# Sixteen blocks of a late modulation, issued from other places of an encoder kernel's first stage

## The chip, the cores and the metric

The kernel runs on one core of a Trainium2 chip. What counts is the device time of one execution in microseconds, the median of several runs. The core has five engines that matter here, each with its own in-order instruction stream: TensorE (PE, with its weight loads as PEld), VectorE (DVE), ScalarE (ACT), GpSimd (POOL) and SyncE (SP), whose queue issues every DMA of this kernel.

## The reference, cut to what matters

An encoder of two layers over 1024 rows of width 1024, in float32. Each layer's input is a normalised x, scaled and shifted by a modulation that comes from one vector c; a gate of the same origin weighs the layer's output:

```
c_act = silu(c)
mod = c_act @ ada_w[i] + ada_b[i]              # one row of 3072 for each layer i
shift, scale, gate = split(mod, 3)
h = rms_norm(x, norm_g[i]) * (1 + scale) + shift
out = layer_ab(h, ...) if i == 0 else layer_diff(h, ...)
x = x + gate * out
```

layer_ab projects h: to a query latent (384 columns) and a key/value latent (256), each of which is normalised later by a row's own root mean square, to a rotary key (32), to queries, keys and values of a stick-breaking attention (512 each) and to gates z (1024). Two attentions follow, then the output projection. Only layer 0's shift and scale are needed at once. Layer 1's shift and scale and both layers' gates are needed much later: they are the late modulation, 4 x 1024 dot products of length 1024, 16 MB of weights.

## The kernel before, in words

Activations lie transposed in SBUF, features on the 128 partitions and 512 rows to a half. Every float32 matrix is split into a high and a low part, and a product is three matmuls (lines 172 to 174): high by high, low by high, high by low. A weight block of 128 output columns is loaded to w_st, cast to w_hi on ACT and its rest taken to w_lo on POOL (wprep, line 153 for the subtraction); dense_fm then runs two halves of 8 x 3 matmuls into a PSUM bank and calls an evacuation. Three score banks (sc) and two dense banks (psd) go round.

The stage around the change, in the order of the code: the first half of the rows is normalised, modulated and multiplied by the five latent blocks (to line 592); then the second half (latent_evac writes both parts of a latent to memory, lat_h and lat_l); the rotary table cs is made on DVE (lines 629 to 636); the rotary key's block (krt, line 698) is projected; the two norms of the latents follow (latent_norm: sums on POOL and PE, an inverse root by Newton steps on DVE, rl in the names, and row_out, which turns the result to a row and writes it: rq_d for the queries, rkv_d for keys and values). The query row is read back to all partitions (rqb), and DVE makes two scaled tables te and to from it and cs, which are written to tq_d. The rotated key is written to krot_d; the code calls this DMA `turned`. Then four gate blocks zb are projected through the score banks, with ACT's sigmoid and a product on DVE (line 250); zb and te share buffers. After that begins the stick-breaking attention: the first query/key block goes to the two dense banks, is split by ACT (qk_a) and DVE (qk_k, line 153), and three DMAs rearrange its halves (qk_b, qk_k, qk_a); meanwhile the values (wv) are projected.

The late modulation is the generator ada_rest: sixteen steps, each of which loads a block of 1 MB (ada_st, two times 1024 columns) into one of six buffers of the tag ld, takes two dots on DVE (line 522, one ISA instruction and the reading of its accumulator) and adds the bias (line 677, into gt for the gates, n = 0, or modc for layer 1's shift and scale, n = 1). `more(n)` advances it by n steps. A scheduler then orders each engine's instructions by its own estimates and the data they depend on. `with tc.issue_after(x):` adds that what the block traces on x's engine stands behind x on that engine; where x is a DMA, it binds DMAs of SP alone, and dots on DVE are not held by it. Before, steps are advanced by four behind `turned` and by four behind each of the first three gate blocks.

Of the kernel before, what the change touches and what calls it, by code (L numbers as in the profile page):

```python
# [21 lines left out]
P = 128  # L22
# [3 lines left out]
NT = S // P  # L26
# [45 lines left out]
def kernel(ctx, tc, a, out):  # L72
    nc = tc.nc
    mm = nc.tensor.matmul

    def dma(dst, src):
        dst = dst.bitcast(F32) if dst.dtype == F32R else dst
        src = src.bitcast(F32) if src.dtype == F32R else src
        return nc.sync.dma_start(dst, src)
# [34 lines left out]
    tq_d = dram.tile([2, P, S], F32, name="tq_d")  # L114
    rq_d = dram.tile([NT, P], F32, name="rq_d")
    rkv_d = dram.tile([NT, P], F32, name="rkv_d")
    krot_d = dram.tile([P, S], F32, name="krot_d")
# [58 lines left out]
    def dense_fm(w, rhs, evac, bank=None):  # L176

        wh, wl = (t.rearrange("p (k c) -> p k c", c=P) for t in w)
        nk = len(rhs)
        for half in range(2):  # L180
            ps = (bank or d_bank)()
            sl = slice(half * 512, half * 512 + 512)
            for k in range(nk):
                mm3(ps, wh[:, k, :], wl[:, k, :], rhs[k][0][:, sl], rhs[k][1][:, sl], k == 0, k == nk - 1)
            evac(ps, half, sl)

    def rstd_cols(pool, ss, n, scale, eps, name, extra=None, bufs=2):

        h, r, t = (pool.tile([P, n], F32, name=name + x, tag=name + x, bufs=bufs) for x in "hrt")
        if extra is None:  # L190
            nc.vector.tensor_scalar(h, ss, scale, eps, op0=ALU.mult, op1=ALU.add)
        else:
            nc.vector.scalar_tensor_tensor(t, extra, eps, extra, op0=ALU.mult, op1=ALU.mult)
            nc.vector.scalar_tensor_tensor(h, ss, scale, t, op0=ALU.mult, op1=ALU.add)
        ri = r.bitcast(I32)
        nc.vector.tensor_scalar(ri, h.bitcast(I32), 1, None, op0=ALU.logical_shift_right)
        nc.vector.tensor_scalar(ri, ri, -1, 0x5F3759DF, op0=ALU.mult, op1=ALU.add)
        nc.vector.tensor_scalar(h, h, -0.5, None, op0=ALU.mult)
        for _ in range(3):
            nc.vector.tensor_mul(t, r, r)  # L200
            nc.vector.tensor_mul(t, t, h)
            nc.vector.scalar_tensor_tensor(r, t, 1.5, r, op0=ALU.add, op1=ALU.mult)
        return r

    def row_out(pool, cols, n, dst, bank):

        tr = bank()
        nc.tensor.transpose(tr[0:n, 0:P], cols, identf)
        row = pool.tile([16, P], F32, name="row", tag="row", bufs=2)
        nc.vector.tensor_copy(row[0:n], tr[0:n, 0:P])  # L210
        dma(dst, row[0:n])

    def row_bc(src, n):

# [14 lines left out]
    def row_sums(tile_of, nt, bank):  # L229

        ps = bank()
        for t in range(nt):
            mm(ps[:, t:t + 1], tile_of(t), ones, start=True, stop=True)  # L233
        return ps[:, 0:nt]
# [242 lines left out]
    with tc.tile_pool(name="a0", bufs=1, reuse_waits="tile") as a0:  # L477
# [10 lines left out]
        def ada_load(k):  # L488
            ada_st[k] = a0.tile([P, 2, D], F32, name="ada_st", tag="ld", bufs=NLD)
            return dma(ada_st[k].rearrange("p i d -> p (i d)"), a["ada_t"][k - 1] if k else a["ada_0"])  # L490

        def wide(name, tag):
            return a0.tile([P, S], F32, name=name, tag=tag, bufs=4)
# [23 lines left out]
        def dots(st):  # L517

            m = a0.tile([P, 2], F32, name="adm", tag="adm", bufs=4)
            for n in range(2):  # L520
                junk = a0.tile([P, D], F32, name="junkd", tag="junkd")
                nc.vector.tensor_tensor_reduce(junk, st[:, n, :], cb, op0=ALU.mult, op1=ALU.add, scale=1.0, scalar=0.0,
                                               accum_out=m[:, n:n + 1])
            return m
# [8 lines left out]
        def x_mod(g, k, xts, lo):  # L533

            tr = t_bank()
            for j in range(4):
                nc.tensor.transpose(tr[:, j * P:(j + 1) * P], xts[j][:, k * P:(k + 1) * P], identf)
            hf = a0.tile([P, 512], F32, name="hf", tag="hf", bufs=3)
            sl = slice(g * 512, g * 512 + 512)
            nc.scalar.activation(hf, tr, AF.Identity, scale=gsc[0][:, k:k + 1], bias=modc[0][:, k:k + 1])  # L540
            hi = nc.scalar.copy(hT[k][0][:, sl], hf)
            return sub(lo, hT[k][1][:, sl], hf, hT[k][0][:, sl].bitcast(F32)), hi
# [38 lines left out]
        for k in range(KC):  # L581
            if k + 1 < KC:
                known = ada_block(k + 1)
                _, done = x_mod(0, k + 1, x0, "vec")
                if k + 4 < KC:
                    held = ada_load(k + 4)
# [22 lines left out]
        for k in range(KC):  # L609
            ready, _ = x_mod(1, k, x1, "vec")  # L610
# [56 lines left out]
        def ada_rest():  # L667
            bias = adab.rearrange("p (i n) -> p i n", n=8)
            for n in range(2):
                dst, b_ = ((gt, bias[:, 2::3, :]), (modc[1], bias[:, 3:5, :]))[n]  # L670
                dst = dst.rearrange("p (i n) -> p i n", n=8)
                for k in range(KC):
                    st = a0.tile([P, 2, D], F32, name="ada_st", tag="ld", bufs=NLD)
                    with tc.issue_after((turned if n or k > 1 else held).ins):
                        dma(st.rearrange("p i d -> p (i d)"), a["ada_r"][n, k])
                    with tc.issue_after(turned.ins):
                        nc.vector.tensor_tensor(dst[:, :, k], dots(st), b_[:, :, k], op=ALU.add)
                    yield k
        rest = ada_rest()

        def more(n):
            for _ in range(n):
                next(rest, None)

        def latent_norm(b0, n, row_d):
            part = lambda half, b: sqt[half, b // 2][:, b % 2 * 512:b % 2 * 512 + 512]
            for half in range(2):
                for b in range(b0 + 1, b0 + n):
                    nc.gpsimd.tensor_tensor(part(half, b0), part(half, b0), part(half, b), op=ALU.add)
            ss = row_sums(lambda t: part(t // 4, b0)[:, t % 4 * P:t % 4 * P + P], NT, v_bank)  # L690
            r = rstd_cols(a0, ss, NT, 1.0 / (n * P), 1e-6, "rl")
            row_out(a0, r, NT, row_d, v_bank)


        krt = wide("krt", "a")
# [3 lines left out]
        with tc.issue_after(held.ins):  # L699
            wkr = wprep(a["w0"][21])  # L700
        dense_fm(wkr, hT, kr_evac, s_bank)
        latent_norm(0, 3, rq_d)
        latent_norm(3, 2, rkv_d)
        rqb = wide("rqb", "b")
        dma(rqb, row_bc(rq_d, P))
# [4 lines left out]
        to = wide("to", "a")  # L710
        nc.vector.tensor_mul(to[0:64], rqb[0:64], cs[0:64])
        nc.vector.tensor_copy(to[64:128], rqb[64:128])
        dma(tq_d[1], to)
        krc = wide("krc", "b")
        for qd in range(4):
            o = qd ^ 1
            nc.scalar.copy(krc[32 * qd:32 * qd + 32], krt[32 * o:32 * o + 32])
        nc.gpsimd.tensor_tensor(krt, krt, krc, op=ALU.add)
        turned = dma(krot_d, krt)
        more(4)  # L720

        for h in range(8):
# [1 line left out]
        for b in range(NZB):  # L724
# [5 lines left out]
            more(4)  # L730
        more(16)
        row_out(a0, gt, 16, gate_d.rearrange("i (n p) -> (i n) p", p=P), t_bank)
        mod_finish(1)

# [141 lines left out]
    for h in range(8):  # L876
# [29 lines left out]
        def mla_mid(par):  # L906
            c1 = slice(4 * par, 4 * par + 4)
            rl = mp.tile([P, 4], F32, name="rl", tag="rl", bufs=2)
            if not seq:
                nc.vector.tensor_tensor(lst[:, 4 * par + 2:4 * par + 4], lst[:, 4 * par + 2:4 * par + 4],  # L910
                                        lst2[:, 2 * par:2 * par + 2], op=ALU.add)
            elif par == 1:
                nc.vector.tensor_tensor(lst[:, 4:8], lst[:, 4:8], lst2, op=ALU.add)
            nc.vector.reciprocal(rl, lst[:, c1])
            row_out(mp, rl, 4, rin_d[h, c1], t_bank)
            rb = mp.tile([P, 512], F32, name="rb", tag="rb", bufs=1)
            dma(halves(rb)[nr[e]], row_bc(rin_d[h, c1], 64))
            z_ = par_view(zt, par, seq)
            nc.gpsimd.tensor_tensor(z_[nr[e]], halves(rb)[nr[e]], z_[nr[e]], op=ALU.mult)
# [206 lines left out]
    with tc.tile_pool(name="e0", bufs=1, reuse_waits="tile") as e0:  # L1126
        fg = e0.tile([P, D], F32, name="fg")
        dma(fg, a["final_g"].to_broadcast([P, D]))
        for t in range(NT):
# [17 lines left out]
            r = rstd_cols(e0, s1, 1, 1.0 / D, 1e-6, "rg")  # L1147
# [93 lines left out]
```

## Time and profile before

| | us |
|---|---|
| median of 3 runs | 1492.08 (1490.76 to 1494.83) |
| the profiled execution | 1493.56 |
| its span | 1491.8 |
| PE busy | 1386.7 (93%) |
| DVE busy | 950.9 (64%) |
| ACT busy | 679.3 (46%) |
| POOL busy | 428.3 (29%) |

The span runs from the first to the last instruction. Busy times are sums over the whole program; what a stage waits for is read from its own stretch. The late modulation lies in the first 190 us: the trace has its dots between 94 and 184 us. "PEclk" is the granted share of TensorE's full clock of 2.4 GHz; 0.5 is its lower level, 1.2 GHz.

### The profile page before, as it was taken

How to read it: one execution, taken by the hardware profiler on the slowest of the kernel's cores; microseconds unless marked ns; L12 is line 12 of the kernel's file. 1: busy time of each engine (PE TensorE's matmuls, PEld its weight loads, DVE VectorE, ACT ScalarE, POOL GpSimd, SP SyncE). 2: the span in 40 equal slices, each digit the busy share in tenths (PEclk: the TensorE clock that was granted, in tenths of full speed). 3: DMA queues.
4: the chain of work that ended last, by engine and by line, in shares of the span. 5: the costliest groups of instructions: out<-in, count | busy, mean ns of one | idle time of the engine just before them, and what ended most of it. 6: DMA issues, size and time to landing. Idle time of an engine off the chain costs nothing.

```text
span 1491.8 us, 20861 instructions
## 1 busy us (share of the span) xinstructions
PE 1386.7 (93%) x7264; PEld 1155.6 (77%) x7264; DVE 950.9 (64%) x2137; ACT 679.3 (46%) x1380; POOL 428.3 (29%) x498
## 2 busy tenths in 40 slices
PE   5999599999998799998879899999999999997797
PEld 4778488888886688887767688888888888886686
DVE  5677947777678865576557426655575656567674
ACT  5742145555555653555345325444444534344321
POOL 2132311322236454635132311132121312134100
PEclk9999899999999999999989999999999999998899
DMA  9536921222243156433746231333232333335262
GB/s 371 225 116 254 365 74 49 67 73 63 62 139 116 58 173 212 145 110 104 238 127 246 57 93 41 78 105 108 64 93 64 101 80 97 85 105 172 81 202 91
DMA packets 110072, 190.38 MB, mean 128 GB/s; under 512 B 8784, under 2 KB 70088, under 8 KB 106896
## 3 DMA queue, kind: packets, MB, share of 16 engines
q1 hardware_dynamic: 109968, 189.05, 40.1%
q8 instruction: 58, 0.95, 0.3%
q14 instruction: 46, 0.38, 0.1%
HBM read 131.75 MB, written 39.27 MB: 115 GB/s over the span
## 4 chain that ended last, share of the span: by engine, by line
PE 39%; DMA 6%; DVE 4%; issue 2%; POOL 2%; ACT 1%; SPq 0%; DVEq 0%; POOLq 0%; ACTq 0%
PE psd L172 7%; PE psd L173 7%; PE psd L174 7%; PE sc L293 4%; PE pv L327 4%; PE sc L172 2%; PE sc L173 2%; PE sc L174 2%; DMA rb<-rst_d 1%; DMA qk_k<-qk_a 1%; DMA w_st<-in_wo_dram 1%; PE pv L233 1%; DMA y_hi<-yh_d 1%; PE tr L307 1%; PE tr L309 1%
## 5 line engine op out<-in xcount | busy, mean ns | idle before, releaser
L153 POOL TENSOR_TENSOR w_lo<-w_st,w_hi 128x1024 fp32r<-128x1024 f32 (+2 forms) x61 | 149.5, 2453 | 369.4 <-ACT w_hi L158 365.5
L153 DVE TENSOR_TENSOR pt_l<-tr,pt_h 128x512 fp32r<-128x512 f32 (+1 forms) x240 | 148.7, 631 | 103.1 <-ACT pt_h L158 90.0
L158 ACT CAST pt_h<-tr 128x512 fp32r<-128x512 f32 (+1 forms) x240 | 125.9, 545 | 131.8 <-PE tr L309 121.4
L174 PE MATMUL psd<-h1h,w_lo 128*128 128x512 f32 x448 | 177.0, 395 | 0.0
L173 PE MATMUL psd<-h1l,w_hi 128*128 128x512 f32 x448 | 176.2, 393 | 0.0
L172 PE MATMUL psd<-h1h,w_hi 128*128 128x512 f32 x448 | 176.0, 393 | 0.0
L172 PE MATMUL psd<-h0h,w_hi 128*128 128x512 f32 x264 | 106.6, 404 | 15.6 <-DVE qk_k L153 15.6
L293 PE MATMUL sc<-qk_k,qk_a 128*128 128x512 f32 (+2 forms) x288 | 104.4, 367 | 2.0 <-DVE st L1056 1.0
L173 PE MATMUL psd<-h0l,w_hi 128*128 128x512 f32 x264 | 106.0, 401 | 0.0
L174 PE MATMUL psd<-h0h,w_lo 128*128 128x512 f32 x264 | 105.1, 399 | 0.0
L158 ACT CAST w_hi<-w_st 128x1024 fp32r<-128x1024 f32 x55 | 57.7, 1050 | 94.3 <-PE psd L173 34.2
L293 PE MATMUL sc<-qk_k,qk_b 128*128 128x512 f32 (+2 forms) x288 | 98.2, 348 | 0.0
L1056 DVE CUSTOM_DVE_ANT_0 g<-sc,tz 128x512 f32<-128x512 f32 (+3 forms) x128 | 72.2, 586 | 40.0 <-PE sc L293 33.9
L173 PEld LDWEIGHTS psd<-h1l,w_hi 128*128 128x128 f32 x448 | 84.2, 188 | 16.9
L174 PEld LDWEIGHTS psd<-h1h,w_lo 128*128 128x128 f32 x448 | 84.2, 188 | 16.2
L172 PEld LDWEIGHTS psd<-h1h,w_hi 128*128 128x128 f32 x448 | 84.2, 188 | 16.1
L1062 ACT ACTIVATE g<-g,st 128x640 f32<-128x640 f32 (+3 forms) x64 | 63.4, 990 | 67.2 <-DVE st L1061 62.4
L327 PE MATMUL pv<-pt_l,vt 128*128 128x256 f32 x320 | 88.7, 303 | 5.1 <-DVE pt_l L153 4.7
L327 PE MATMUL pv<-pt_h,vt 128*128 128x256 f32 x320 | 89.4, 296 | 2.7 <-DVE ot L417 2.7
L776 DVE TENSOR_TENSOR_SCAN g<-g 128x640 f32<-128x640 f32 (+3 forms) x32 | 65.8, 2056 | 20.4 <-ACT g L773 20.4
L172 PEld LDWEIGHTS psd<-h0h,w_hi 128*128 128x128 f32 x264 | 50.5, 191 | 25.6 <-DVE qk_k L153 16.1
L327 PEld LDWEIGHTS pv<-pt_l,vt 128*128 128x128 f32 x320 | 62.6, 196 | 9.1 <-DVE pt_l L153 4.8
(458 smaller groups left out, 3736.5 us busy)
## 6 DMA issues: line engine op xcount, KB each, us to landing
w_st<-in_w_dram SPq DMA_DIRECT2D x43, 512.0 KB
ada_st<-in_ada_r_dram SPq DMA_DIRECT2D x16, 1024.0 KB
w_st<-in_wo_dram SPq DMA_DIRECT2D x16, 512.0 KB
ada_st<-in_ada_t_dram SPq DMA_DIRECT2D x7, 1024.0 KB
yh_d<-yh SPq DMA_DIRECT2D x28, 256.0 KB
yl_d<-yl SPq DMA_DIRECT2D x28, 256.0 KB
w_st<-in_wv_dram SPq DMA_DIRECT2D x12, 512.0 KB
qk_b<-qk_k SPq DMA_DIRECT2D x24, 256.0 KB
```

Of the source, the lines that this page charges most:

```text
L153: return (nc.vector if eng == "vec" else nc.gpsimd).tensor_tensor(out_, x_, y_, op=ALU.subtract)
L158: nc.scalar.copy(hi, src)
L172: mm(ps, sh, mh, start=start, stop=False)
L173: mm(ps, sh, ml, start=False, stop=False)
L174: mm(ps, sl, mh, start=False, stop=stop)
L233: mm(ps[:, t:t + 1], tile_of(t), ones, start=True, stop=True)
L293: mm(ps[:, :nn], st[:, q], mv[:, lo_:lo_ + nn], start=m == 0, stop=not diag and m == len(pairs) - 1)
L307: nc.tensor.transpose(tr[:, P:256], pb[:, (2 * j + 1) * P:(2 * j + 2) * P], identf)
L327: mm(dst, st, tt[w][:, m * 256:m * 256 + 256], start=j == 0 and m == 0 and x == 0, stop=j == n - 1 and m == 1 and x == len(ps_) - 1)
L776: nc.vector.tensor_tensor_scan(ur, ur, ur, 1.0, op0=ALU.mult, op1=ALU.bypass)
L1056: nc.vector.tensor_tensor_reduce(e_[:, sl], ps, tz[:, S - L + sl.start:S - L + sl.stop], op0=ALU.add, op1=ALU.max, scale=1.0, scalar=-3e38 ...
L1062: nc.scalar.activation(e_[:, :L], e_[:, :L], AF.Exp, scale=0.125, bias=st[:, 2 + c:3 + c], accum_out=lst[:, c1:c1 + 1] if c == 0 else st[: ...
```

## The change

Four of the sixteen steps are advanced ahead of the norms, where before none was. Their loads stand behind `held` (the last load of layer 0's modulation) and their adds behind `ready` (the last product of the second half's modulated input, on DVE). The other four of n = 0 have their loads behind the write of the query norm's row (`row_st`), and the eight of n = 1 behind the second table's write (`scaled`); the adds of all twelve stand behind the copy of the query norm's row (`row_cp`), which is on DVE. row_out returns these two instructions.

```diff
--- before.py
+++ after.py
@@ -207,8 +207,7 @@
         tr = bank()
         nc.tensor.transpose(tr[0:n, 0:P], cols, identf)
         row = pool.tile([16, P], F32, name="row", tag="row", bufs=2)
-        nc.vector.tensor_copy(row[0:n], tr[0:n, 0:P])
-        dma(dst, row[0:n])
+        return nc.vector.tensor_copy(row[0:n], tr[0:n, 0:P]), dma(dst, row[0:n])
 
     def row_bc(src, n):
 
@@ -671,9 +670,9 @@
                 dst = dst.rearrange("p (i n) -> p i n", n=8)
                 for k in range(KC):
                     st = a0.tile([P, 2, D], F32, name="ada_st", tag="ld", bufs=NLD)
-                    with tc.issue_after((turned if n or k > 1 else held).ins):
+                    with tc.issue_after((held if n == 0 and k < 4 else row_st if n == 0 else scaled).ins):
                         dma(st.rearrange("p i d -> p (i d)"), a["ada_r"][n, k])
-                    with tc.issue_after(turned.ins):
+                    with tc.issue_after((ready if n == 0 and k < 4 else row_cp).ins):
                         nc.vector.tensor_tensor(dst[:, :, k], dots(st), b_[:, :, k], op=ALU.add)
                     yield k
         rest = ada_rest()
@@ -681,6 +680,8 @@
         def more(n):
             for _ in range(n):
                 next(rest, None)
+
+        more(4)
 
         def latent_norm(b0, n, row_d):
             part = lambda half, b: sqt[half, b // 2][:, b % 2 * 512:b % 2 * 512 + 512]
@@ -689,7 +690,7 @@
                     nc.gpsimd.tensor_tensor(part(half, b0), part(half, b0), part(half, b), op=ALU.add)
             ss = row_sums(lambda t: part(t // 4, b0)[:, t % 4 * P:t % 4 * P + P], NT, v_bank)
             r = rstd_cols(a0, ss, NT, 1.0 / (n * P), 1e-6, "rl")
-            row_out(a0, r, NT, row_d, v_bank)
+            return row_out(a0, r, NT, row_d, v_bank)
 
 
         krt = wide("krt", "a")
@@ -699,7 +700,7 @@
         with tc.issue_after(held.ins):
             wkr = wprep(a["w0"][21])
         dense_fm(wkr, hT, kr_evac, s_bank)
-        latent_norm(0, 3, rq_d)
+        row_cp, row_st = latent_norm(0, 3, rq_d)
         latent_norm(3, 2, rkv_d)
         rqb = wide("rqb", "b")
         dma(rqb, row_bc(rq_d, P))
@@ -710,13 +711,13 @@
         to = wide("to", "a")
         nc.vector.tensor_mul(to[0:64], rqb[0:64], cs[0:64])
         nc.vector.tensor_copy(to[64:128], rqb[64:128])
-        dma(tq_d[1], to)
+        scaled = dma(tq_d[1], to)
         krc = wide("krc", "b")
         for qd in range(4):
             o = qd ^ 1
             nc.scalar.copy(krc[32 * qd:32 * qd + 32], krt[32 * o:32 * o + 32])
         nc.gpsimd.tensor_tensor(krt, krt, krc, op=ALU.add)
-        turned = dma(krot_d, krt)
+        dma(krot_d, krt)
         more(4)
 
         for h in range(8):
```

What becomes of it on the engines, by the built programs. Line numbers after the change are one lower up to line 682 and one higher behind it.

DVE, around the end of the latents: lat_l is the low part of the last latent block, krt the rotary key's two halves, rlh the first step of the query norm; an ISA pair on junkd and adm is one dot. Before:

```order
L522 ISA junkd,adm<-ada_st,cb 128x1024
L522 ISA adm 128x1
L605 SCALAR_TENSOR_TENSOR lat_l<-sc,smalls,lat_h 128x512
L677 TENSOR_TENSOR gt<-adm,smalls 128x2
L698 TENSOR_TENSOR krt<-sc,cs 128x512 x2
L191 TENSOR_SCALAR rlh<-pv 128x8
```

And now:

```order
L521 ISA junkd,adm<-ada_st,cb 128x1024
L521 ISA adm 128x1
L604 SCALAR_TENSOR_TENSOR lat_l<-sc,smalls,lat_h 128x512
L676 TENSOR_TENSOR gt<-adm,smalls 128x2
L521 ISA junkd,adm<-ada_st,cb 128x1024
L521 ISA adm 128x1
L699 TENSOR_TENSOR krt<-sc,cs 128x512
L521 ISA junkd,adm<-ada_st,cb 128x1024
L521 ISA adm 128x1
L676 TENSOR_TENSOR gt<-adm,smalls 128x2
L699 TENSOR_TENSOR krt<-sc,cs 128x512
```

Before, one block's last dot and its gate product stand ahead of the last latent product here; now further dots, of the next two blocks, stand around it and around the two halves of krt, ahead of the norm.

DVE, from the query norm's row to the first gate product (row, te, to, zb as above). Before:

```order
L210 COPY row<-pv 8x128
L707 COPY te<-rqb 64x1024
L708 TENSOR_TENSOR te<-rqb,cs 64x1024
L711 TENSOR_TENSOR to<-rqb,cs 64x1024
L712 COPY to<-rqb 64x1024
L191 TENSOR_SCALAR rlh<-pv 128x8
L250 TENSOR_TENSOR zb<-zb,sc 128x512 x2
```

And now, with nine rows of the second block's dots and the second norm's steps left out:

```order
L210 COPY row<-pv 8x128
L521 ISA junkd,adm<-ada_st,cb 128x1024
L521 ISA adm 128x1
L191 TENSOR_SCALAR rlh<-pv 128x8
L521 ISA junkd,adm<-ada_st,cb 128x1024
L521 ISA adm 128x1
...
L201 TENSOR_TENSOR rlt<-rlt,rlh 128x8
L708 COPY te<-rqb 64x1024
L709 TENSOR_TENSOR te<-rqb,cs 64x1024
L712 TENSOR_TENSOR to<-rqb,cs 64x1024
L713 COPY to<-rqb 64x1024
L249 TENSOR_TENSOR zb<-zb,sc 128x512
```

Two blocks' dots and six steps of the second norm came in between the row and te, and the second of the first two zb moved off its neighbour.

SP, from the query norm's row on (rq_d), with the read to all partitions (rqb), the tables' writes (tq_d) and the rotated key's (krot_d); in_w is any weight block of the projections. Before:

```order
L79 DMA w_st<-in_w_dram 128x1024
L79 DMA rq_d<-row 8x128
L79 DMA rqb<-rq_d 128x1024
L79 DMA tq_d<-te 128x1024
L79 DMA tq_d<-to 128x1024
L79 DMA krot_d<-krt 128x1024
L79 DMA ada_st<-in_ada_r_dram 128x2048 x2
```

And now:

```order
L79 DMA w_st<-in_w_dram 128x1024
L79 DMA rq_d<-row 8x128
L79 DMA ada_st<-in_ada_r_dram 128x2048 x2
L79 DMA rqb<-rq_d 128x1024
L79 DMA ada_st<-in_ada_r_dram 128x2048 x2
L79 DMA krot_d<-krt 128x1024
L79 DMA w_st<-in_w_dram 128x1024
L79 DMA tq_d<-te 128x1024
L79 DMA tq_d<-to 128x1024
L79 DMA ada_st<-in_ada_r_dram 128x2048 x2
L79 DMA zs_d<-zb 128x1024
```

Four block loads stand ahead of the tables' writes, two of them ahead of rqb, and the rotated key's write and a weight load went in front of the tables too.

## Rows read from the trace of the kernel before

**Rows 1.** Waits of PE over the whole span: total us, times, longest.

```profile
PE psd L172 <- DVE qk_k L153: 15.6, 1, 15.6
```

**Rows 2.** Windows around the stall: width, busy us and instructions by engine, PEclk, DMA share, GB/s.

```profile
core 0: us, PE busy (x) PEld busy (x) DVE busy (x) ACT busy (x) POOL busy (x), PEclk, DMA share, GB/s
130.00:157.70 27.70, 27.46 (x121) 22.64 (x122) 23.91 (x48) 4.88 (x7) 5.90 (x2) 1.00 1.01 397
...
169.00:184.60 15.60, 0.04 (x1) 0.04 (x1) 14.94 (x29) 2.02 (x3) 5.42 (x7) 0.64 0.77 305
184.60:198.80 14.20, 14.20 (x53) 11.54 (x53) 0.50 (x1) 1.01 (x2) 0.00 (x0) 0.79 0.48 127
```

**Rows 3.** Timeline of PE: start us, us, line, operation, idle before and releaser.

```profile
130.24 0.50 PE L172 MATMUL sc<-h0h,w_hi 128*128 128x512 f32 x1 [0.75 <-DVE zb L250]
...
168.52 0.39 PE L174 MATMUL psd<-h0h,w_lo 128*128 128x512 f32 x1
...
184.56 0.80 PE L172 MATMUL psd<-h0h,w_hi 128*128 128x512 f32 x1 [15.65 <-DVE qk_k L153]
...
198.72 0.47 PE L293 MATMUL sc<-qk_k,qk_a 128*128 128x512 f32 x1
```

**Rows 4.** Timeline of DVE from the end of the latents to the stall's end.

```profile
110.33 0.69 DVE L698 TENSOR_TENSOR krt<-sc,cs 128x512 f32<-128x512 f32 x1 [5.30 <-PE sc L174]
...
118.61 0.28 DVE L210 COPY row<-pv 8x128 f32<-8x128 f32 x1 [0.68 <-PE pv L208]
...
123.98 2.11 DVE L707 COPY te<-rqb 64x1024 f32<-64x1024 f32 x1 [5.09 <-DMA rqb<-rq_d]
...
129.50 1.29 DVE L250 TENSOR_TENSOR zb<-zb,sc 128x512 f32<-128x512 f32 x2
...
136.60 1.23 DVE L522 CUSTOM_DVE_ANT_0 junkd<-ada_st,cb 128x1024 f32<-128x1024 f32 x1 [3.24 <-DMA ada_st<-in_ada_r_dram]
...
137.87 3.29 DVE L522 CUSTOM_DVE_ANT_0 junkd<-ada_st,cb 128x1024 f32<-128x1024 f32 x1
...
162.82 1.21 DVE L522 CUSTOM_DVE_ANT_0 junkd<-ada_st,cb 128x1024 f32<-128x1024 f32 x1
...
165.42 1.22 DVE L522 CUSTOM_DVE_ANT_0 junkd<-ada_st,cb 128x1024 f32<-128x1024 f32 x1
...
183.82 1.28 DVE L153 TENSOR_TENSOR qk_k<-psd,qk_a 128x512 fp32r<-128x512 f32 x2
```

**Rows 5.** Timeline of SP's queue: when DMAs were issued.

```profile
118.92 0.30 SPq L79 DMA_DIRECT2D rq_d<-row  x1
120.17 0.34 SPq L79 DMA_DIRECT2D rqb<-rq_d  x1
...
130.15 2.02 SPq L79 DMA_DIRECT2D ada_st<-in_ada_r_dram  x2
...
185.16 0.54 SPq L79 DMA_DIRECT2D qk_b<-qk_k  x1
...
193.61 0.46 SPq L79 DMA_DIRECT2D qk_a<-qk_a  x1
```

**Rows 6.** Timeline of POOL beside the tables and the first late dots.

```profile
123.19 2.35 POOL L153 TENSOR_TENSOR w_lo<-w_st,w_hi 128x1024 fp32r<-128x1024 f32 x1 [5.28 <-ACT w_hi L158]
136.96 3.12 POOL L153 TENSOR_TENSOR w_lo<-w_st,w_hi 128x1024 fp32r<-128x1024 f32 x1 [11.42 <-ACT w_hi L158]
```

**Rows 7.** Windows of 2 us behind a short stand of PE.

```profile
728.00:730.00 2.00, 0.54 (x2) 0.50 (x3) 0.00 (x0) 0.00 (x0) 0.00 (x0) 0.95 1.17 346
730.00:732.00 2.00, 2.00 (x7) 1.62 (x7) 0.27 (x1) 0.00 (x0) 0.00 (x0) 0.50 0.80 298
732.00:734.00 2.00, 2.00 (x10) 1.85 (x10) 1.11 (x3) 1.17 (x2) 0.30 (x1) 0.70 0.04 15
```

**Rows 8.** Timeline of ACT ahead of the stall's end.

```profile
173.43 1.04 ACT L158 CAST w_hi<-w_st 128x1024 fp32r<-128x1024 f32 x1 [13.88 <-DMA w_st<-in_w_dram]
174.38 1.07 ACT L158 CAST qk_a<-psd 128x512 fp32r<-128x512 f32 x2
```

## The prediction

> **What bounds the kernel now.** I read the waits first, then the windows, then the timeline of each engine around the change. PE is busy 93% of the span, so the time moves where PE stands still or runs at the lower clock. The waits of PE have one row that towers over the others: 15.6 us, in one piece, for the split of the first query/key block (qk_k, line 153) on DVE [rows 1]. The windows show what surrounds it: from 130 to 157.7 us PE is full and the DMA engines are too (397 GB/s); from 169.0 to 184.6 PE does nothing while DVE is busy for 14.9 of 15.6 us; from 184.6 to 198.8 PE is full again but at a granted clock of 0.79 [rows 2]. The PE timeline puts edges on it: the last matmul before the stall starts at 168.52, so PE is done at about 168.75; the next starts at 184.56; the first scores of the stick-breaking attention start at 198.72 [rows 3]. So DVE is what ends last here. Its timeline shows why: behind the query row's scaling (te, 123.98) and the first gate products (zb, 129.50) it works through fourteen blocks of the late modulation, two dots and an add each, from 136.60 on, and only then comes qk_k at 183.82 [rows 4]. A block takes 2.60 us (162.82 to 165.42). Before that DVE had holes: 5.30 us ahead of the second krt product, 5.09 ahead of te, 3.24 ahead of the first late dot [rows 4]. The SP queue tells why the dots were late: these blocks are issued from 130.15 on, behind the writes of te, to and krt, while the norm's row left at 118.92 [rows 5].
>
> **The change, part by part.** Nothing is computed differently; sixteen blocks stay sixteen.
>
> *Two more blocks among the latents.* Blocks 3 and 4 (four dots and two adds on DVE: 2 x 2.60 = 5.2 us) now stand around the last latent product and the two krt products. The hole there is 5.30 us [rows 4], so they cost nothing if they have landed; their loads go out during the second half's latents. If the cover fails, the second krt product and the first norm behind it slip; the excess of 5.2 us over the hole is at most 0 to 1 us, and I take 0.
>
> *Twelve blocks behind the query norms.* The first two loads now follow the norm's row, at about 119.3 instead of 130.15. The nearest landing is that of rqb: issued 120.17, used at 123.98, that is 3.8 us for 0.5 MB [rows 4, 5]; a block of 1.05 MB has another 0.5 MB at about 0.41 MB/us [rows 2], 1.25 us, so it lands at about 124.4 (bounds 123 to 126). From there DVE has no hole left. Its end moves by the two blocks that left (5.2) and by the hole ahead of the first late dot (3.24): 183.82 - 5.2 - 3.24 = 175.4 for the start of qk_k. Bounds: the number of POOL splits beside its dots can differ by one or two, each worth about 2 us [rows 4, 6], so 173 to 179.
>
> *What is put ahead of the gate products.* On DVE the dots of two of these blocks now stand ahead of te, to and the first zb. PE needs this zb: three score banks go round, and already before it waited 0.75 us at 130.24 for it [rows 3]. The first dot starts at 124.4 instead of te at 123.98 (+0.4). Beside POOL's split from 123.19 to 125.54 the te copy took 2.11 us, against some 0.7 without, and a dot beside the split from 136.96 to 140.08 took 3.29 and ended 1.1 behind it [rows 4, 6]; so the dot that now stands in te's place ends at about 126.7, 1.1 late, and te loses its 1.4. With two blocks (5.2) and four small steps of the second norm (0.8) between, the first zb ends 0.4 + 1.1 - 1.4 + 5.2 + 0.8 = 6.1 us later. PE's wait of 0.75 becomes about 6.9, and all that PE does up to the stall moves by 6.1. Bounds: 4 (no stop beside POOL, early landing) to 8 (rqb, now queued behind two blocks, lands later than the dots end).
>
> The Trainium skill, page "SBUF — State Buffer", section "SBUF: two separate sides", says that a VectorE operation with two SBUF inputs and a GpSimd operation that reads SBUF hold a shared port pair exclusively, the second waiting until the first is through. By that rule the first new dot is stopped, and this is the 6.1; without it the shift would be 5.0 and the forecast 1.1 us lower. The 3.29 us dot agrees.
>
> *The clock.* Behind the long stall 0.21 of 14.2 us were lost to the lower level, 1.2 GHz: 3.0 us [rows 2]. A much shorter stand of PE at 728 us was followed by clocks of 0.95, 0.50 and 0.70 in slices of 2 us: 0.1 + 1.0 + 0.6 = 1.7 us [rows 7]. The new wait of 6.9 us lies between them: 1.7 to 3.0, and I take 2.2; 0 is the lower bound, if the fall misses it.
>
> *Where PE and DVE meet.* PE is done with the query/key block at 168.75 + 6.1 + 2.2 = 177.0. Then ACT makes its next weight cast (1.04) and the first half of qk_a (0.54), and DVE the first half of qk_k (0.64) [rows 4, 8]: 2.2 us, so PE goes on at 179.2. DVE's own 175.4 + 0.64 = 176.0 is earlier: PE, not DVE, is late next. Before it was 184.56: 5.4 us won. From there before took 14.2 us to the scores (198.72 - 184.56), 3.0 of them lost to the clock. Now a stall of 2.2 us may cost 0 to 1.7 of clock (0.9), and the three copies of the halves, which began at 185.16 with the last issued at 193.61 [rows 5], have a weight load of 0.5 MB between them (0 to 1.25 us, 0.6). Both run beside each other, the longer counts: the copies need 0.65 + 8.45 + 2.9 (the landing, as from the second's issue to the last's) + 0.6 = 12.6. So 14.2 - 12.6 = 1.6 more.
>
> Sum: 5.4 + 1.6 = 7.0 us. All behind 198.72 keeps its order but for a handful of PE rows near the end, which I cost at 0 (bounds -1 to +1). The profiled execution took 1493.56 (span 1491.8 and 1.8 around it): 1486.6. The median of the runs lies 1.5 below it: 1485.1.
>
> **The rivals.**
> - *The stall goes whole.* 15.65 + 3.0 = 18.6, 1473.5. For it: the blocks start 11 us earlier. Against: DVE alone needs until 175.4, and the order puts dots ahead of the zb that PE waits for. Chance 0.04.
> - *DVE is late, PE is not.* The wait for zb stays at 4 and costs no clock: PE is done at 172.8, DVE's 176.0 decides, 8.6 won there and 1.6 to 2.2 behind: about 10.5, 1481.5 (down to 1479 with fewer stops beside POOL). Chance 0.17.
> - *The wait for zb eats the gain.* A shift of 8 or more and 3.0 of clock: 168.75 + 11 + 2.2 = 182.0, 2.6 won and 0.5 to 1.5 behind: 3 to 4, 1488.5, which is within what can be told from no change. For it: rqb stands behind two blocks; ACT and DVE take turns on the gates. Against: the two blocks' transfers (5 us) end before their dots do. Chance 0.16.
> - *Slower: SP starves the dots.* SP issues in order, and the last eight blocks now stand behind the writes of te and to, which wait for DVE, which waits for dots. If a block came every 3.9 us instead of 2.6, DVE would end 12 x 1.3 = 15.6 us later, at 191: with no clock won back that is 1498 to 1500. Slower by 4.5 us begins at 8.6 + 4.5 = 13.1 us over twelve blocks, 3.7 us a block, some 280 GB/s, against 397 now [rows 2]. Against: te's write goes out at about 134, a block lands 5 us later, and DVE still has four blocks in hand until 146. Chance 0.07.
>
> **How the numbers follow.** 0.3% of the median, 4.5 us, is about what a measurement of this kernel can tell from no change. The forecast has 0.56, for 1483 to 1487.5; faster is 0.56 + 0.17 + 0.04 = 0.77, the same 0.16, slower 0.07. The range for 8 in 10 reaches down to the lower end of the second rival and up over the third: 1479 to 1491.
>
> **What would show it.** In the profile after: PE's wait for qk_k falls from 15.6 to about 2 (0 to 4), and a wait of sc for zb near 130 us grows from 0.7 to about 7; the first late dot starts near 124.4 and qk_k between 175 and 179; the hole ahead of the second krt product closes; the clock is below 1 shortly behind 136; the scores start near 191.7. I am wrong if te starts before the dots' end, if zb's wait is below 3 or above 10, if dots wait for loads behind 140 us, or if the end moves by other than the scores' start.

## The result, and the profile after

The changed kernel took 1485.06 us as the median of 8 runs (1477.64 to 1491.69), the kernel before 1492.08 beside it: ratio 0.9942, 95% interval 0.9923 to 0.9962. Run again in three more sets it gave 1482.91, 1482.69 and 1486.31, with ratios of 0.9952, 0.9950 and 0.9957. So it is faster by 0.4 to 0.6%, 5 to 7 us. Its profiled execution was the fastest of the first eight, 1477.64 (span 1475.9); that one is read here, and its stage turned out to be the same in three later profiles.

The waits of PE, as [rows 1]: the 15.6 us for qk_k have become 2.2, and the wait for zb, 0.75 in [rows 3], is now 5.8.

```profile
PE sc L172 <- DVE zb L249: 5.8, 1, 5.8
...
PE psd L172 <- DVE qk_k L153: 2.2, 1, 2.2
```

The windows around both waits, columns as in [rows 2]. PE stands still from 129.6 (135.40 less 5.80) to 135.4, runs four microseconds at 0.50 of the clock (1.2 GHz), then 36.6 us full; behind the second, short stand its clock is 1.00, where in [rows 2] it was 0.79.

```profile
130.00:135.40 5.40, 0.00 (x0) 0.00 (x0) 5.31 (x10) 0.00 (x0) 0.00 (x0) 0.74 1.00 398
135.40:139.40 4.00, 4.00 (x9) 3.13 (x10) 4.00 (x12) 0.60 (x1) 0.00 (x0) 0.50 1.05 427
139.40:176.00 36.60, 36.56 (x162) 29.71 (x160) 31.09 (x58) 6.02 (x9) 10.20 (x9) 1.00 0.82 326
176.00:178.10 2.10, 0.00 (x0) 0.00 (x0) 0.72 (x2) 1.83 (x3) 1.17 (x1) 1.00 0.89 304
178.10:189.50 11.40, 11.38 (x52) 9.41 (x53) 0.56 (x1) 0.92 (x2) 1.21 (x1) 1.00 0.47 118
```

The timeline of PE, as [rows 3]: the query/key block ends at 175.96 (178.12 less 2.16) instead of 168.91 (184.56 less 15.65), PE goes on at 178.12 instead of 184.56, and the scores start at 189.51 instead of 198.72.

```profile
135.40 0.79 PE L172 MATMUL sc<-h0h,w_hi 128*128 128x512 f32 x1 [5.80 <-DVE zb L249]
...
178.12 0.50 PE L172 MATMUL psd<-h0h,w_hi 128*128 128x512 f32 x1 [2.16 <-DVE qk_k L153]
...
189.51 0.47 PE L292 MATMUL sc<-qk_k,qk_a 128*128 128x512 f32 x1
```

The timeline of DVE, as [rows 4]. Read it from the top: the hole ahead of krt is down to 0.21 and the norm's row leaves 0.11 us later than before; the first late dot starts at 124.44 and takes 2.29; te waits for the dots until 130.76 and then costs 0.68 instead of 2.11; zb comes at 134.66 instead of 129.50. At 177.38 DVE has been idle for 3.14 us and waits for ACT: it is no longer the late one.

```profile
110.44 0.69 DVE L699 TENSOR_TENSOR krt<-sc,cs 128x512 f32<-128x512 f32 x1 [0.21 <-PE sc L174]
...
118.72 0.28 DVE L210 COPY row<-pv 8x128 f32<-8x128 f32 x1 [0.68 <-PE pv L208]
...
124.44 2.29 DVE L521 CUSTOM_DVE_ANT_0 junkd<-ada_st,cb 128x1024 f32<-128x1024 f32 x1 [5.44 <-DMA ada_st<-in_ada_r_dram]
...
126.77 1.23 DVE L521 CUSTOM_DVE_ANT_0 junkd<-ada_st,cb 128x1024 f32<-128x1024 f32 x1
...
130.76 0.68 DVE L708 COPY te<-rqb 64x1024 f32<-64x1024 f32 x1
...
134.66 0.69 DVE L249 TENSOR_TENSOR zb<-zb,sc 128x512 f32<-128x512 f32 x1
...
167.71 3.30 DVE L521 CUSTOM_DVE_ANT_0 junkd<-ada_st,cb 128x1024 f32<-128x1024 f32 x1
...
177.38 1.29 DVE L153 TENSOR_TENSOR qk_k<-psd,qk_a 128x512 fp32r<-128x512 f32 x2 [3.14 <-ACT qk_a L158]
```

POOL's splits beside two of these dots: the dots of 2.29 and 3.30 us (ending at 126.73 and 171.01) end 1.09 and 1.08 us behind the splits that they start in (125.64 and 169.93), while the dot at 126.77 takes 1.23.

```profile
123.29 2.35 POOL L153 TENSOR_TENSOR w_lo<-w_st,w_hi 128x1024 fp32r<-128x1024 f32 x1 [5.28 <-ACT w_hi L158]
...
166.59 3.34 POOL L153 TENSOR_TENSOR w_lo<-w_st,w_hi 128x1024 fp32r<-128x1024 f32 x1 [9.15 <-ACT w_hi L158]
```

SP's queue, as [rows 5]. The three copies of the halves were issued from 178.73 to 185.45, 6.7 us from first to last, where [rows 5] has 8.45. The reads of the key/value norm's row and of the rotated key (rkv and two of kr_t, 1 MB together) were issued from 173.66 on, 5.1 us ahead of the first copy.

```profile
119.02 0.30 SPq L79 DMA_DIRECT2D rq_d<-row  x1
...
120.28 0.38 SPq L79 DMA_DIRECT2D rqb<-rq_d  x1
...
173.66 0.32 SPq L79 DMA_DIRECT2D rkv<-rkv_d  x1
...
178.73 0.54 SPq L79 DMA_DIRECT2D qk_b<-qk_k  x1
...
185.45 0.47 SPq L79 DMA_DIRECT2D qk_a<-qk_a  x1
```

### The profile page after: what moved, and what is told of

Same layout as the page of the kernel before. It is cut to its first block, busy times and chain, and to the rows that moved or that the text cites. A ratio compares the mean times of both kernels' runs of the same rounds, so it can differ in the third digit from the quotient of the medians.

```text
span 1475.9 us, 20859 instructions
## 1 busy us (share of the span) xinstructions
PE 1381.9 (94%) x7264; PEld 1152.1 (78%) x7264; DVE 944.6 (64%) x2137; ACT 679.3 (46%) x1380; POOL 428.1 (29%) x498
## 4 chain that ended last, share of the span: by engine, by line
PE 41%; DVE 4%; DMA 4%; issue 2%; ACT 1%; POOL 1%; SPq 0%; DVEq 0%; ACTq 0%; POOLq 0%
PE psd L172 8%; PE psd L173 8%; PE psd L174 8%; PE sc L292 4%; PE pv L326 4%; PE sc L172 2%; PE sc L173 2%; PE sc L174 2%; DMA y_hi<-yh_d 1%; PE pv L232 1%; DMA w_st<-in_wo_dram 1%; PE tr L306 1%; PE tr L308 1%; PE tr L307 1%; DMA xp_d<-xr 1%
## 5 line engine op out<-in xcount | busy, mean ns | idle before, releaser
L174 PE MATMUL psd<-h1h,w_lo 128*128 128x512 f32 x448 | 177.0, 395 | 0.0
L326 PEld LDWEIGHTS pv<-pt_h,vt 128*128 128x128 f32 x320 | 63.3, 198 | 10.2 <-DVE ot L416 4.1
```

The source lines that it names most:

```text
L174: mm(ps, sl, mh, start=False, stop=stop)
L326: mm(dst, st, tt[w][:, m * 256:m * 256 + 256], start=j == 0 and m == 0 and x == 0, stop=j == n - 1 and m == 1 and x == len(ps_) - 1)
```

## The experiments

Profiles differ by up to 1.4 us ahead of the stage, so times are also told from the start of the norm's row copy on DVE (118.61 in [rows 4]'s kernel, 118.72 after). From there to the scores the kernel before takes 80.1 us, the changed one 70.8.

**The kernel before and the changed one, once more.**

> The kernel before, for a second profile of it. If what the executions differ in lies behind the scores' start (as between the two profiles of the changed kernel), the stage is as in the first one: PE stands 15.4 to 15.8 us behind the query/key block, scores at 198 to 200, and the span is 1487 to 1492.

> The changed kernel as it is, a second profile of it, since its eight runs lay 14 us apart (1477.6 to 1491.7) and the profiled one was the lowest of them. Theory A (the stage between 119 and 190 us is the same in every execution, and the executions differ in what comes after): PE's wait for zb 5 to 7 us, PE goes on behind qk_k at 177 to 180, scores of the stick-breaking attention start at 189 to 191 as in the first profile, and the rest of the span differs. Theory B (the stage itself differs, by the clock behind the wait for zb or by transfers): scores start anywhere between 189 and 198, and the span differs by as much. Median again 1483 to 1487, ratio 0.993 to 0.997.

> The changed kernel a third time. Scores at 189 to 190 again; the rest of the span differs by up to 10 us between the profiles, in 700 to 840 and 1290 to 1420 us, where PE's stands of 1 to 3 us are or are not followed by half clock. Median 1482 to 1486.

The kernel before, second profile (span 1488.4): the stand is the same, 15.72 us, and the scores come 12.71 us behind it instead of 14.16, since less clock was lost. From row copy to scores: 197.59 - 118.86 = 78.7 against 80.1. The forecast of 198 to 200 was missed by 0.4.

```profile
184.88 0.80 PE L172 MATMUL psd<-h0h,w_hi 128*128 128x512 f32 x1 [15.72 <-DVE qk_k L153]
...
197.59 0.48 PE L293 MATMUL sc<-qk_k,qk_a 128*128 128x512 f32 x1
```

The changed kernel, second profile (span 1481.3): both waits (5.84 and 2.16) and the scores (189.40) within 0.2 us of the first, as theory A had it; the third (1479.3) and the fourth (1486.5, e12 below) likewise, 5.80, 2.16 and scores at 189.69 and 190.06. The medians of e1 and e12 missed what was expected of them by 0.1 and 0.3 us.

So the stage saves 78.7 - 71.1 = 7.6 to 80.1 - 70.8 = 9.3 us in every pair of profiles, and the 10 us by which the spans of the changed kernel differ lie behind it. The windows of the first and then of the fourth profile (columns as in [rows 2]) show one place where PE's clock fell in one and not in the other, 1.00 against 0.93.

```profile
765.00:840.00 75.00, 66.87 (x322) 51.15 (x321) 47.77 (x95) 34.69 (x51) 22.99 (x19) 1.00 0.43 146
```

```profile
765.00:840.00 75.00, 66.54 (x308) 51.36 (x307) 47.74 (x95) 31.59 (x48) 20.16 (x17) 0.93 0.42 146
```

**Only the first part (e2), only the second (e3).**

```diff
e2: four blocks among the latents, the twelve held as before
-  with tc.issue_after((held if n == 0 and k < 4 else row_st if n == 0 else scaled).ins):
+  with tc.issue_after((held if n == 0 and k < 4 else turned).ins):
-  with tc.issue_after((ready if n == 0 and k < 4 else row_cp).ins):
+  with tc.issue_after((ready if n == 0 and k < 4 else turned).ins):
-  dma(krot_d, krt)
+  turned = dma(krot_d, krt)
e3: two blocks among the latents as before, fourteen begun behind the norm
-  (held if n == 0 and k < 4 else ...)   (ready if n == 0 and k < 4 else row_cp)   more(4)
+  (held if n == 0 and k < 2 else ...)   (ready if n == 0 and k < 2 else row_cp)   more(2)
```

> Only the first part: four blocks among the latents, the other twelve behind the tables' and the rotated key's writes as before. Theory A (DVE's end sets where PE goes on; the hole in front of krt takes the two blocks for nothing): krt and the norm's row stay (110.4, 118.7), te back at 124.0, wait for zb below 1, dots again from 136.6, qk_k at 183.82 - 5.2 = 178.6, PE stands 168.75 to 179.4 (10.6 us), half clock behind it, scores at 192 to 193.5, median 1485 to 1487. Rival (the earlier start of the twelve is what pays): scores at 197 to 199, 1490 to 1492. Rival (the four crowd the norm): row copy behind 119.5, everything later, 1490 or more.

> Only the second part: two blocks among the latents as before, the other fourteen begun behind the query norm. Theory A: wait for zb as in the changed kernel, 5 to 7; PE done with the query/key block at 175 to 177; DVE's dots end two blocks (5.2 us) behind the changed kernel's 174.2, at 179.4; so here DVE is late and PE goes on at 180 to 181, scores at 191.5 to 193, median 1486 to 1488. Rival (PE is late in any case, two blocks more on DVE cost nothing): PE goes on at 178, scores 189.5, as the changed kernel. Rival (the wait for zb eats all): scores at 196 or more, 1490 to 1492.

e2: 1486.47 us, ratio 0.9970 (0.9958 to 0.9981). DVE's timeline: the first late dot waits for its block until 138.30, 1.7 us later than in [rows 4], and qk_k follows at 180.14 with no idle time in front, so DVE is late. PE stands 11.60 us instead of the 10.6 expected, and the scores, at 193.96, missed 192 to 193.5 by 0.5.

```profile
138.30 2.49 DVE L521 CUSTOM_DVE_ANT_0 junkd<-ada_st,cb 128x1024 f32<-128x1024 f32 x1 [4.62 <-DMA ada_st<-in_ada_r_dram]
...
180.14 1.28 DVE L153 TENSOR_TENSOR qk_k<-psd,qk_a 128x512 fp32r<-128x512 f32 x2
```

e3: 1486.88 us, ratio 0.9985 (0.9977 to 0.9994). PE stands twice, 5.80 for zb and 6.01 for qk_k, and both times goes on at the lower clock (0.79 us for a matmul that takes 0.50 at 178.12 above). The scores came at 197.86, not at 191.5 to 193: qk_k started on DVE 2.5 us later than two blocks explain (182.93, in a profile that starts 1.0 late), and the second fall of the clock, which I had not counted, took most of the rest.

```profile
136.39 0.79 PE L172 MATMUL sc<-h0h,w_hi 128*128 128x512 f32 x1 [5.80 <-DVE zb L249]
...
183.67 0.79 PE L172 MATMUL psd<-h0h,w_hi 128*128 128x512 f32 x1 [6.01 <-DVE qk_k L153]
...
197.86 0.47 PE L292 MATMUL sc<-qk_k,qk_a 128*128 128x512 f32 x1
```

From row copy to scores e2 takes 75.0 and e3 78.2. Against 78.7 to 80.1 before that is 3.7 to 5.1 and 0.5 to 1.9, together less than the 7.6 to 9.3 of both parts. Each part alone leaves DVE late, PE with a stand of 6 us or more at qk_k and a fallen clock behind it (13.1 and 14.2 us to the scores, against 11.4); only both make PE the late one.

**The wait for zb taken away (e4).**

```diff
-  dma(rqb, row_bc(rq_d, P))
+  spread = dma(rqb, row_bc(rq_d, P))
-  nc.vector.tensor_copy(to[64:128], rqb[64:128])
+  tabled = nc.vector.tensor_copy(to[64:128], rqb[64:128])
-  (held if n == 0 and k < 4 else row_st if n == 0 else scaled)   (... else row_cp)
+  (held if n == 0 and k < 4 else spread if n == 0 else scaled)   (... else tabled)
```

> The changed kernel, with rqb's transfer ahead of the first block loads and the twelve blocks' dots behind the tables te and to on DVE. Theory A (PE and DVE are nearly level at the meeting point; taking away the wait for zb moves the wait to qk_k): te at 124.0, wait for zb 0 to 2.5, PE done at 169 to 171, DVE's dots end at 174 to 176, PE goes on at 175 to 177 after a stand of 5 to 7, half clock behind that one instead, scores at 187.5 to 190: 0 to 2 us better than the changed kernel, median 1483 to 1485. Rival (the wait for zb is the whole remaining loss): scores at 183 to 185, 1478 to 1480. Rival (the loads are late without the early start): dots wait for loads, DVE ends behind 178, worse than the changed kernel.

1483.90 us, ratio 0.9950 (0.9931 to 0.9968), the changed kernel 1482.91 in the same set. The wait for zb is back at 0.75 and PE finishes its block early; then it stands 6.42 us at qk_k, at the lower clock behind it. Row copy to scores: 71.9, 1.1 more than with the wait. So the wait for zb is not what is left of the loss; it stands in front of an equal one. Scores at 191.64 - 1.0 missed 187.5 to 190 by 0.6.

```profile
131.33 0.50 PE L172 MATMUL sc<-h0h,w_hi 128*128 128x512 f32 x1 [0.75 <-DVE zb L249]
...
177.94 0.80 PE L172 MATMUL psd<-h0h,w_hi 128*128 128x512 f32 x1 [6.42 <-DVE qk_k L153]
...
191.64 0.47 PE L292 MATMUL sc<-qk_k,qk_a 128*128 128x512 f32 x1
```

**DVE's hole filled (e5), and both (e6).** DVE idles 5.44 us ahead of 124.44. Here blocks 5 and 6 are loaded early and their dots fill it.

```diff
e5:
-  (held if n == 0 and k < 4 else row_st if n == 0 else scaled)
+  (held if n == 0 and k < 6 else row_st if n == 0 else scaled)
e6: as e4, and
+  (held if n == 0 and k < 6 else spread if n == 0 else scaled)
+  (ready if n == 0 and k < 4 else row_cp if n == 0 and k < 6 else tabled)
```

> The changed kernel, but the loads of blocks 5 and 6 go out early too (behind the same early load as the first four), so that their dots can fill the hole of 5.4 us that DVE has ahead of 124.4; blocks 7 and 8 then come ahead of te, as 5 and 6 do in the changed kernel. Theory A (with the wait for zb as it is, PE is late at qk_k and not DVE): te starts at 130 to 132 as now, wait for zb 5 to 8, DVE's dots end about 5 us earlier (169), yet PE goes on at 177.5 to 180, scores at 189 to 191.5, median within 2 us of the changed kernel. Rival (DVE's work is what counts): PE goes on at 172 to 174, scores at 184 to 186, 1477 to 1480.

> Both at once: blocks 5 and 6 loaded early and their dots in the hole ahead of 124, rqb's transfer ahead of the other loads, and the ten blocks left behind the tables on DVE. Theory A (PE's wait for zb and DVE's end are two limits, nearly level, and only taking from both moves the meeting point): te at 124 to 126, wait for zb 1 to 3, DVE's dots end at 170 to 172 instead of 176 in the run with the tables first, PE goes on at 173 to 175, scores at 184.5 to 187, that is 2.5 to 5 us ahead of the changed kernel; median 1479 to 1482. Rival (loads arrive late, since eight of them now stand behind the second table's write): dots wait for loads by more than 2 us together, PE goes on behind 176, no better than the run with the tables first.

e5: 1480.33 us, ratio 0.9928 (0.9906 to 0.9950), the changed kernel 1482.69 (0.9950) in the same set: not told apart. The median lies 2.4 below it, where within 2 was expected. The wait for zb grew to 7.53. At qk_k PE didn't wait at all: other matmuls stand there now in PE's order, ahead of the scores. Row copy to scores 71.5, against 70.8; with that work already done, the first matmul of the projection from ckh comes 331.0 us behind the row copy against 332.1 to 335.4 in the four profiles of the changed kernel. So DVE's filled hole bought about one microsecond as far as this measure tells, nearer to theory A than to the rival.

```profile
138.15 0.79 PE L172 MATMUL sc<-h0h,w_hi 128*128 128x512 f32 x1 [7.53 <-DVE zb L249]
...
191.21 0.40 PE L292 MATMUL sc<-qk_k,qk_a 128*128 128x512 f32 x1
```

e6: 1481.20 us, ratio 0.9931 (0.9907 to 0.9955); scores 68.7 behind the row copy, 2.1 ahead of the changed kernel. The scores missed 184.5 to 187 by 0.5 even with the profile's 1.0 taken off. The wait for zb was 4.01, not 1 to 3: SP's queue shows rqb issued 3.93 us behind rq_d, against 1.26 in the changed kernel. Eight copies of the relative-position rows (rel_d), held up by the two blocks loaded before them, were being issued until 120, just ahead of the row's write; SP then waited 3.6 us for that write to land.

```profile
114.00 5.99 SPq L79 DMA_DIRECT2D rel_d<-rel_r  x8
...
120.67 0.30 SPq L79 DMA_DIRECT2D rq_d<-row  x1
...
124.60 0.33 SPq L79 DMA_DIRECT2D rqb<-rq_d  x1
```

**SP cleared (e9), SP starved (e10).** Both start from e6. In e9 the eight copies are issued behind the last block's load, in e10 right behind the tables' writes.

```diff
+  with tc.issue_after(last[0].ins):      # e9; e10: scaled.ins
       dma(rel_d[h], rel_r[h:h + 1, :].to_broadcast([24, NREL]))
```

> The run with the hole filled and the tables first, and in addition the eight copies of the relative-position rows (rel_d, 6 us of SP's queue, which there stood ahead of the norm's row because rel_r landed behind the two blocks) moved behind the last block's load. Theory A (rqb was late there only because SP was busy with these): rqb issued about 1.3 us behind rq_d instead of 3.9, te at 124 to 126 against a row copy at 118.7, wait for zb 1 to 2, DVE's dots end at 168 to 171, PE goes on behind qk_k at 172 to 174, scores at 183 to 186: 3 to 6 us ahead of the changed kernel, median 1476 to 1481. Rival (rqb is late because of the block transfers beside it): te at 126 or later, scores at 187 or more, no better than without the move.

> As the run before, but the eight copies (6 us of SP's queue) stand right behind the tables' writes and ahead of the eight last block loads. It tests the rival of the prediction by which SP starves the dots: with loads from about 134.5 on instead of 128.5, and two blocks in hand until about 135, DVE should wait some 4 to 6 us for its next block near 140, its dots end at 173 to 176, and PE go on at 175 to 177: 3 us behind the run before. Other theory (the loads have slack, DVE doesn't wait): no hole for ada_st behind 130, PE goes on as in the run before.

> The best kernel so far (hole filled, tables first, the relative-position copies late) beside the changed kernel on one chip. Theory A: stage as in its first profile, PE goes on behind qk_k at 173 to 175 and scores at 186 to 188, 2.5 to 3.5 us ahead of the changed kernel; median 1477 to 1481, 2 to 5 us below it. Whether half clock follows the stand of 2.2 us again: if it is fixed by what PE does before, the first matmul behind it takes 0.8 us again and the scores come 12.9 us later; if it is chance, 11.4 in one of the two. Rival: the lead in the stage is given back behind 190 us, medians within 1 us.

> The changed kernel beside it, for the comparison on one chip: scores at 189 to 190, the stand at qk_k 2.2 us with full clock behind it (first matmul 0.5 us), median 1481 to 1486.

e9: 1478.56 us, ratio 0.9906 (0.9876 to 0.9937). rqb leaves 1.23 us behind rq_d (SP waited 0.9 us for the write to land), the wait for zb is 1.77, and PE goes on at 173.84; the scores miss 186 by 0.7, since half clock followed the stand.

```profile
119.05 0.29 SPq L79 DMA_DIRECT2D rq_d<-row  x1
...
120.28 0.32 SPq L79 DMA_DIRECT2D rqb<-rq_d  x1
```

```profile
131.41 0.50 PE L172 MATMUL sc<-h0h,w_hi 128*128 128x512 f32 x1 [1.77 <-DVE zb L249]
...
173.84 0.80 PE L172 MATMUL psd<-h0h,w_hi 128*128 128x512 f32 x1 [2.16 <-DVE qk_k L153]
...
186.74 0.47 PE L292 MATMUL sc<-qk_k,qk_a 128*128 128x512 f32 x1
```

Again, beside the changed kernel (e11, e12): 1478.33 us against 1486.31, ratios 0.9923 (0.9894 to 0.9952) and 0.9957 (0.9935 to 0.9980) to the kernel before. The medians lie 8.0 us apart, more than the 2 to 5 expected and more than the stage explains. e9 and e11, one kernel, have the lowest medians of all versions, though the intervals of e5, e6 and e10 overlap theirs; in the stage they are 0.7 and 3.0 us ahead of e6. The stand at qk_k was even longer in e11, 3.04, and this time full clock followed: scores 65.7 us behind the row copy instead of 68.0, earlier than the 186 to 188 expected and 2.8 to 5.1 ahead of the changed kernel.

```profile
131.88 0.50 PE L172 MATMUL sc<-h0h,w_hi 128*128 128x512 f32 x1 [1.77 <-DVE zb L249]
...
173.58 0.50 PE L172 MATMUL psd<-h0h,w_hi 128*128 128x512 f32 x1 [3.04 <-DVE qk_k L153]
...
184.96 0.48 PE L292 MATMUL sc<-qk_k,qk_a 128*128 128x512 f32 x1
```

e10: 1479.85 us, ratio 0.9919 (0.9890 to 0.9948), within the spread of e9. DVE did wait for a block, but once and for 3.28 us, short of the 4 to 6 expected; what it cost showed elsewhere: PE waited 2.31 and 1.74 us for a weight block whose load had stood behind the same copies and the six block loads that follow them. Scores 71.5 behind the row copy, 3.5 later than in e9 (PE's order is that of e5; at the projection from ckh it is 331.7 against 329.0, 2.7 later, no more than this measure scattered by in the changed kernel).

```profile
146.18 1.22 DVE L521 CUSTOM_DVE_ANT_0 junkd<-ada_st,cb 128x1024 f32<-128x1024 f32 x1 [3.28 <-DMA ada_st<-in_ada_r_dram]
```

```profile
162.56 0.67 PE L172 MATMUL psd<-h0h,w_hi 128*128 128x512 f32 x1 [2.31 <-ACT w_hi L158]
...
166.25 0.80 PE L174 MATMUL psd<-h0h,w_lo 128*128 128x512 f32 x1 [1.74 <-POOL w_lo L153]
...
191.30 0.39 PE L292 MATMUL sc<-qk_k,qk_a 128*128 128x512 f32 x1
```

## Why the prediction was right, point by point

- *Two more blocks among the latents cost nothing*: right. The hole of 5.30 closed to 0.21 and the row's copy moved by 0.11.
- *First dot at 124.4, 1.1 late beside POOL*: right, 124.44, ending at 126.73 (forecast 126.7; the rate in [rows 2] is 0.40 MB/us, not 0.41, which moves the landing by under 0.1). The rule of the Trainium skill, page "SBUF — State Buffer", section "SBUF: two separate sides", agrees: the two dots shown beside POOL's splits, and a third (145.01, 2.49 us), start inside a split and end 1.1 us behind it. te, now clear of the split, takes 0.68.
- *The first zb 6.1 us later*: 5.16 (134.66 - 129.50). The term of 0.8 for the second norm's small steps was wrong; from 126.77 to te at 130.76 three dots, an add and five such steps take 3.99, that is 1.33 a dot where half a block of 2.60 is 1.30, so the steps hide between the dots. The rest is te and what follows it up to zb, 3.90 instead of 5.52, where I had counted a gain of 1.4.
- *2.2 us of clock behind the wait*: right in size, 0.50 of 4.0 us, 2.0.
- *PE, not DVE, late next; 2.2 us of ACT and DVE between*: right. PE was done at 175.96 (forecast 177.0, from 168.75, where [rows 3] have 168.52 + 0.39 = 168.91), stood 2.16, went on at 178.12 (179.2); DVE had 3.14 us to spare. e2 and e3 show what else it would have been, and e4 that the two limits are nearly level.
- *12.6 us from there to the scores*: 11.39. This term failed most. I had the copies as the longer of two parts, at 12.6, and PE's own work at 14.2 - 3.0 + 0.9 = 12.1. PE's work ended the stretch, 11.38 of 11.40 us busy, as it had before (14.20 of 14.20 [rows 2]); no clock was lost where I had 0.9, so 2.8 was won instead of 1.6. The copies took 0.61 + 6.72 + 2.9 = 10.2 by the same sum (whose 0.65 is 0.60 in [rows 3, 5]). I carried the 8.45 us between them over from the kernel before. There the second waited 5.0 us for the first to land, and 1 MB, rkv and kr_t, had been issued 1.8 us ahead of the first; now these go out when DVE's dots end, 5.1 us ahead of it, and that wait is 1.9. In the five profiles that have them at most 2.3 us ahead, first and last copy lie 8.2 to 9.0 apart, in the nine others 6.0 to 6.7. The clock doesn't set this: 6.07 in e9, where half clock followed the stand, 6.51 in e11, at full.

```profile
183.32 0.33 SPq L79 DMA_DIRECT2D rkv<-rkv_d  x1
183.70 0.90 SPq L79 DMA_DIRECT2D kr_t<-krot_d  x2
...
190.71 0.50 SPq L79 DMA_DIRECT2D qk_k<-qk_a  x1
```

- *Sum 7.0 at the scores*: 9.2 between the two first profiles, 7.6 to 9.3 over all of them.
- *Nothing behind the scores*: neither shown nor refuted. From the scores to PE's last matmul the four profiles of the changed kernel span 10 us (1278 to 1288) and the two of before, 1282 and 1285, lie inside. One of the prediction's signs of being wrong, an end that moves by other than the scores' start, did show in the first pair of profiles: the end moved by 15.9 us there, the scores by 9.2. That the median came out at 1485.06 against 1485.1 is therefore luck: the stage won more than I said, and the runs gave less than the stage, 4.9 to 7.4 where the profiles have 7.6 to 9.3. Whether that is the scatter of the clock's falls behind it or something lost there I can't settle.
- *SP starves the dots* didn't happen: behind 124.44 no dot of the changed kernel waits for a load. e10 provoked it, for one wait of 3.28 us, and there PE waited longer for late weights, 4.05 us in all.

## What to carry to other kernels

Where two engines meet, write down when each is ready and move the later one; once they are level, a shorter wait on one side only reappears on the other (e4), and a gain needs both sides (e9). Before you move loads ahead, read what stands behind them in the issuing queue: two early blocks delayed a small transfer by 2.7 us, through eight copies that nobody needed yet (e6 against e9). Judge such a change by its stage in a profile beside the runs: the changed kernel's stage repeated to 0.3 us where the runs of one set were up to 15 us apart. Take more than one profile of each version all the same: in this stage the two of the kernel before differ by 1.4 us, and e9 and e11, one kernel, by 2.3.

## What the runs showed that I had not expected

The clock behind a short stand of PE is not set by the stand's length alone. In e9 half clock followed 2.16 us, in e11, the same kernel, full clock followed 3.04 (windows, columns as in [rows 2]: 0.60 against 1.00), and in all four profiles of the changed kernel full clock followed 2.16. The Trainium skill, page "TensorE: Matmul & The Clock Gate", section "Part 1: The HAM clock gate", says of a kernel's start that one kernel shows different numbers of slow matmuls from run to run; these two profiles show the like in the middle of one.

```profile
173.80:178.00 4.20, 4.16 (x12) 3.35 (x13) 0.58 (x1) 0.00 (x0) 3.25 (x7) 0.60 0.76 228
```

```profile
173.50:178.00 4.50, 4.42 (x19) 3.68 (x20) 0.62 (x2) 0.00 (x0) 3.32 (x7) 1.00 0.78 242
```
